# The first two token tiles' norm weights applied at the PSUM exit, and the last block's squares moved to row tiles

## The chip, the cores and the metric

The kernel runs on one NeuronCore of a Trainium2 chip, as one launch. The metric is the device time in microseconds, the median of several runs of the same program. Beside those runs one execution was recorded by the hardware profiler; its rows carry the argument. TensorE multiplies matrices into PSUM, VectorE (DVE in the rows) and ScalarE (ACT) take results out of PSUM and prepare operands, GpSimd (POOL) works on SBUF, and SyncE (SP) issues most of the transfers.

## The reference

One encoder layer over 2048 tokens of width 1024, in fp32, with root-mean-square norms around every part. Cut to what matters here:

```python
def rms_norm(x, g):
    y = xf * lax.rsqrt(jnp.mean(xf * xf, axis=-1, keepdims=True) + RMS_EPS)
    return (y * g.astype(jnp.float32)).astype(x.dtype)
...
u = rms_norm(h, g_mix_pre[l])
z = u @ w_in[l]
...
u = rms_norm(h, g_ffn_pre[l])
y = (jax.nn.silu(u @ w_gate[l]) * (u @ w_up[l])) @ w_down[l]
h = h + rms_norm(y, g_ffn_post[l])
```

Between the two quoted parts stand sliding-window attention, a gated linear recurrence, an output projection and a cross-attention into 256 memory tokens. The change touches the first norm (`g_mix_pre`) at the start of the kernel and the last norm (`g_ffn_post`) at its end.

## The kernel before

**Numbers.** Each fp32 operand of a product is split in two parts that TensorE multiplies fast: "hi" is the value rounded by a copy, "lo" is the value minus hi. A product is then three matmuls: hi by hi, hi by lo, lo by hi (lines 1131 to 1133). So each tile that enters a product costs one copy (ScalarE or GpSimd, line 987 or 989) and one subtraction on VectorE (line 990).

**The start (`in_first`).** The first products are the input projection of 512 tokens. Tokens come in tiles of 128 rows, `x0_0` tiles 0 to 3 and `x0_1` tiles 4 to 7. For each tile, `scaled` calls `normed`: ScalarE squares the rows and sums them (line 429; the squares go to a scratch tile), GpSimd makes the reciprocal root in two small instructions (lines 102 and 104), and VectorE multiplies the tile by it and by the norm weights, which lie broadcast over 128 partitions in the tile `g` (line 431). Then TensorE transposes the tile in eight pieces of 128x128 into two PSUM banks (`flipped`, line 480), after which the model width lies on the partitions. `first` takes the two banks out: ScalarE writes hi (line 497), VectorE lo (line 498). `copied` writes the plain transposed values to `raw` as well (line 486, ScalarE), because a later step of the block product (sums of quarters) needs them unsplit. Meanwhile TensorE turns over the identity matrix (`turns`, line 449), 36 times before tile 0 and 18 times before tile 1. The first products (of kind "q") take tiles 0 and 1 together, 256 columns a matmul, then tiles 2 and 3.

SyncE's queue at the start is: tile 0, the broadcast weights, tile 1, two pieces of the first projection weights (`sraw`), tiles 2 and 3, two more pieces of weights, tiles 4 and 5, and so on.

**The middle.** Block products of 2x2 blocks of 512 columns with seven products instead of eight (`seven`: the steps are numbered 1, 5, 6, 3, 7, 2, 4), an addend kept in a "part" tile (three buffers of 128x512), and operands that stream in from HBM.

**The end (`down_block`).** The last product of the feed-forward part makes 256 tokens at a time, two row tiles of 128x1024 in four halves (i, j). In the last block (`end`), `out` does for each half: an addition out of PSUM (lines 1721 to 1723), a sum of squares on ScalarE (`mean_square`, line 1504, with its scratch tile taken from the same three "part" buffers), and a multiplication by the norm weights on VectorE (line 1730). When both halves of a row tile are there, GpSimd adds the two sums (line 1733) and takes the root (line 1736), VectorE multiplies and adds the residual in two halves (line 1739), and each half is stored.

**Order.** The code is traced in program order, and the framework then lists each engine's instructions in the order in which a simulation of the kernel finds them ready; dependences become semaphore waits. `queued(...)` and `traced(...)` pin the start's order by hand: what stands in the block is issued after the named instruction. In the built program's list the four halves at the end leave PSUM in the order (0,0), (0,1), (1,1), (1,0), while ScalarE squares them in the order (0,1), (1,1), (0,0), (1,0).

Tiles of 128x1024 of the late stages come from a pool with twelve buffers (`row_tile`); small constants come from the pool `cst`, which lies below all other tiles of its side.

Of the kernel before, what the change touches and what calls it, by code (L numbers as in the profile page):

```python
# [11 lines left out]
F32 = mybir.dt.float32  # L12
F32R = mybir.dt.float32r
I32 = mybir.dt.int32
AF = mybir.ActivationFunctionType
ALU = mybir.AluOpType
AX = mybir.AxisListType

P = 128
# [5 lines left out]
KT = D // P  # L25
# [5 lines left out]
EPS = 1e-6  # L31
# [5 lines left out]
def f32(ap):  # L37
    return ap.bitcast(F32)
# [10 lines left out]
class Layer:  # L49
# [372 lines left out]
        self._n += 1  # L422
        return self.st_pool.tile([P, 2, D], F32, tag="pair", name=f"pair_{self._n}", bufs=5)

    def normed(self, x, junk, *at):
        nc = self.nc
        ss = self.small("n_s")
        with self.queued(*at):
            nc.scalar.activation(junk, x, AF.Square, accum_out=ss)
            r = self.rstd([ss], D, "n")  # L430
            nc.vector.scalar_tensor_tensor(x, x, r, self.g_mix, ALU.mult, ALU.mult)

    def traced(self, engine):

# [16 lines left out]
    def in_first(self):  # L451

        nc, I = self.nc, self.I
        stage = []

        def x_loads(s, tiles):
            if tiles[0] == 0:
                stage.append(self.tb.tile([P, 4, D], F32, tag="T", name=f"x0_{s}", bufs=3))
            for i in tiles:
                self.load(stage[s][:, i, :], I["x"][(4 * s + i) * P:(4 * s + i + 1) * P, :])  # L460
                if s + i == 0:
                    self.g_mix = self.gain(I["g_mix_pre"])

        x_loads(0, (0, 1))
        T, raw = {}, {}
        key = {(0, 0): 1, (1, 0): 2, (0, 1): 8, (1, 1): 3}

        def scaled(s, i, *at):
            junk = stage[0][:, i % 2, :] if s else raw[0, 1].rearrange("p k t -> p (k t)")[:, 0:D]
            self.normed(stage[s][:, i, :], junk, *at)  # L470

        def flipped(s, i, kinds):

            x = stage[s][:, i, :]
            banks = []
            for q in range(2):
                ps = self.bank(kinds[q])
                for j in range(4):
                    k = 4 * q + j
                    nc.tensor.transpose(ps[:, j * P:(j + 1) * P], x[:, k * P:(k + 1) * P], self.ident)  # L480
                banks.append(ps.rearrange("p (j t) -> p j t", j=4))
            return banks

        def copied(s, i, banks):
            for q in range(2):
                nc.scalar.activation(raw[q, s][:, :, i * P:(i + 1) * P], banks[q], AF.Copy)

        def parts(s, i, q):
            o = slice(i * P, (i + 1) * P)
            return T[key[q, s]][:, 0, :, o], T[key[q, s]][:, 1, :, o]  # L490

        def first(i, kinds):

            banks = flipped(0, i, kinds)
            for q in range(2):
                hi, lo = parts(0, i, q)
                nc.scalar.activation(hi, banks[q], AF.Copy)
                nc.vector.tensor_tensor(lo, banks[q], f32(hi), ALU.subtract)
            return banks

        def later(i, *at):
            scaled(1, i, *at)
            banks = flipped(1, i, ("sh", "gt")[i % 2])
            copied(1, i, banks)
            for q in range(2):
                self.split2(raw[q, 1][:, :, i * P:(i + 1) * P], *parts(1, i, q), "P")
# [10 lines left out]
        def fetch():  # L517
            for s in range(2):
                for q in range(2):
# [8 lines left out]
        tokens = [[] for _ in range(len(self.ORDER) + 1)]  # L528
        blocks = [("s",) + self.in_block(*p, tokens[i], tokens[i + 1], beside[i + 1], get if i > 9 else (), i < 2,
                                         None if i else lambda: x_loads(0, (2, 3)))  # L530
                  for i, p in enumerate(self.ORDER)]

# [4 lines left out]
        PE, ACT, DVE, POOL = (getattr(mybir.EngineType, e) for e in ("PE", "Activation", "DVE", "Pool"))  # L537
        next(phases)
        self.turns("h", 36)
        x_loads(1, (0, 1))  # L540
        scaled(0, 0)
        b0 = first(0, "sh")
        a0 = self.traced(ACT)
        with self.queued(self.traced(PE)):
            self.turns("g", 18)
        scaled(0, 1)
        with self.queued(self.traced(POOL), self.traced(DVE)):
            next(phases)
        b1 = first(1, "gt")
# [3 lines left out]
        x_loads(1, (2, 3))  # L553
        scaled(0, 2, a0, v1)
        scaled(0, 3, a1)
        with self.queued(self.traced(ACT)):
            copied(0, 0, b0)
        b2 = first(2, "gt")
        a2 = self.traced(ACT)
        with self.queued(self.traced(PE)):  # L560
# [1 line left out]
        b3 = first(3, "sh")  # L562
# [1 line left out]
        with self.queued(self.traced(PE)):  # L564
            next(phases)
        with self.queued(a3):
            for i, b in ((1, b1), (2, b2), (3, b3)):
                copied(0, i, b)
        with self.queued(a3, v3):
            next(phases)  # L570
# [15 lines left out]
        for s in range(2):  # L586
            u.append([])
            for q in range(2):
                self._n += 1
                t = self.big.tile([P, 2, 4, 512], F32R, tag="big", name=f"u1_{q}{s}")  # L590
                r = second[q, s]
# [905 lines left out]
        return lambda kind: self.streamed(lambda t, j: self.load(  # L1497
            t, src[n:n + 2, j].rearrange("i p c -> p i c")), 4, kind, "A", tiles=True, blocked=True)

    def mean_square(self, a, to):  # L1500

        self._n += 1
        junk = self.st_pool.tile([P, 512], F32, tag="part", name=f"junk_{self._n}", bufs=3)
        self.nc.scalar.activation(junk, a, AF.Square, scale=float(D) ** -0.5, accum_out=to)  # L1504

    def mean_squares(self, y, i, ss):
# [186 lines left out]
    def down_block(self, c, f0, nk, n):  # L1693
        nc = self.nc
        last = f0 + 2 * nk == NFF
        end = last and n == NT - 2
        late = last and n >= NT - 4
        y, x, ss = {}, {}, []

        def stream(kind):  # L1700
            if late:
                for i in range(2):
                    y[i] = self.rows_of(self.y2_d, n + i)
            if last and n == 0:
                self.g_post = self.gain(self.I["g_ffn_post"])
            return self.streamed(lambda t, j: self.load(
                t, self.h_d[f0 + j * nk:f0 + (j + 1) * nk, :, n * P:(n + 2) * P].rearrange("k p t -> p k t")),
                nk, kind, "A")

        def part(i, j):  # L1710
            return y[i][:, j * 512:(j + 1) * 512]

        def out(i, j, a, b):
            if i not in y:
                y[i] = self.row_tile()
            if end and not x:
                for r in range(2):
                    x[r] = self.rows_of(self.h2_d, n + r)
            d = part(i, j)
            if b is not None:  # L1720
                nc.vector.tensor_tensor(d, a, b, ALU.add)  # L1721
            elif late:
                nc.vector.tensor_tensor(d, a, d, ALU.add)
            else:
                nc.scalar.activation(d, a, AF.Copy)
            if end:
                if not ss:
                    ss.append(self.small("q_s", 4))
                self.mean_square(d, ss[0][:, 2 * i + j:2 * i + j + 1])
                nc.vector.tensor_tensor(d, d, self.g_post[:, j * 512:(j + 1) * 512], ALU.mult)  # L1730
                if (i, 1 - j) in seen:
                    v = self.small("p_v")
                    nc.gpsimd.tensor_scalar(v, ss[0][:, 2 * i:2 * i + 1], ss[0][:, 2 * i + 1:2 * i + 2], EPS,
                                            ALU.add, ALU.add)
                    r = self.small("p_r")
                    nc.gpsimd.tensor_tensor(r, v, self.mhalf[:, 0:1], ALU.pow)
                    for q in range(2):
                        sl = slice(q * 512, (q + 1) * 512)
                        nc.vector.scalar_tensor_tensor(y[i][:, sl], y[i][:, sl], r, x[i][:, sl], ALU.mult, ALU.add)
                        self.store(self.out[(n + i) * P:(n + i + 1) * P, sl], y[i][:, sl])  # L1740
                seen.append((i, j))

        seen = []

        def after():
            if end:
                return
            s2 = self.small("q_s", 4) if last else None
            for i in range(0 if late else 2):
                if not c:  # L1750
                    self.store(self.y2_d[(n + i) * P:(n + i + 1) * P, :], y[i])
                elif last:
                    self.add(y[i], self.y2_d, n + i)
                else:
                    self.add_to(self.y2_d, n + i, y[i])
                yield
            if last:
                if not late:
                    yield
                for i in range(2):  # L1760
                    self.mean_squares(y[i], i, s2)
                yield
                r = self.rstds(s2)
                for i in range(2):
                    nc.vector.scalar_tensor_tensor(y[i], y[i], r[:, i:i + 1], self.g_post, ALU.mult, ALU.mult)
                    self.add_to(self.out, n + i, y[i])
                    yield

        return stream, out, after, part if late else None


# [19 lines left out]
```

## Time and profile before

| | |
|---|---|
| median of 3 runs | 2552.73 us (2552.61 to 2555.01) |
| the profiled execution, its own time | 2550.01 us |
| its span | 2548.3 us, 34324 instructions, granted clock 0.997 |
| TensorE busy | 2504.8 us, 98% of the span |
| VectorE busy | 1792.1 us, 70% |
| ScalarE busy | 1261.6 us, 50% |
| GpSimd busy | 364.6 us, 14% |
| moved by DMA | 486.33 MB, mean 191 GB/s |

A row of the profile gives the engine, the line of the code, the operation, the tiles it writes and reads by their names in the program, the shapes, and the time. "Idle before" is the time in which the engine had nothing to do, followed by the instruction or the transfer that ended it. Matmuls overlap in the array, so one lasts longer than the distance to the next. A busy engine that nobody waits for costs nothing, and an idle one that is not the last to be ready doesn't either.

### The profile page before, as it was taken

How to read it: one execution, taken by the hardware profiler on the slowest of the kernel's cores; microseconds unless marked ns; L12 is line 12 of the kernel's file. 1: busy time of each engine (PE TensorE's matmuls, PEld its weight loads, DVE VectorE, ACT ScalarE, POOL GpSimd, SP SyncE). 2: the span in 40 equal slices, each digit the busy share in tenths (PEclk: the TensorE clock that was granted, in tenths of full speed). 3: DMA queues.
4: the chain of work that ended last, by engine and by line, in shares of the span. 5: the costliest groups of instructions: out<-in, count | busy, mean ns of one | idle time of the engine just before them, and what ended most of it. 6: DMA issues, size and time to landing. Idle time of an engine off the chain costs nothing.

```text
span 2548.3 us, 34324 instructions
## 1 busy us (share of the span) xinstructions
PE 2504.8 (98%) x12006; PEld 2092.8 (82%) x12006; DVE 1792.1 (70%) x2871; ACT 1261.6 (50%) x2635; POOL 364.6 (14%) x540
## 2 busy tenths in 40 slices
PE   9999999999999999999999999999999999999998
PEld 8878888877997778878878888888888888878886
DVE  8885488987556989988876555576566557574766
ACT  5553466655555566566753333353333335443543
POOL 4231234321311112102200000000000000000022
PEclk9999999999999999999999999999999999999999
DMA  6455655865887996867954522254465434564786
GB/s 201 146 165 178 192 154 170 230 204 146 259 292 275 316 335 189 274 206 226 333 200 146 177 91 87 74 203 148 160 210 195 144 117 159 180 188 106 228 177 151
DMA packets 387885, 486.33 MB, mean 191 GB/s; under 512 B 22272, under 2 KB 283392, under 8 KB 387712
## 3 DMA queue, kind: packets, MB, share of 16 engines
q1 hardware_dynamic: 381664, 462.12, 55.9%
q0 software_dynamic: 6048, 22.02, 5.0%
q8 instruction: 94, 1.54, 0.2%
q14 instruction: 79, 0.65, 0.1%
HBM read 317.34 MB, written 166.72 MB: 190 GB/s over the span
## 4 chain that ended last, share of the span: by engine, by line
PE 51%; DVE 2%; DMA 1%; issue 1%; ACT 1%; POOL 0%; SPq 0%; DVEq 0%; POOLq 0%; ACTq 0%
PE psm L1133 17%; PE psm L1131 17%; PE psm L1132 17%; DVE T L990 0%; DVE S L990 0%; ACT junk L1504 0%; PE pss L1390 0%; DMA out_dram<-row 0%; DMA row<-d_s 0%; DMA row<-in_w_down_dram 0%; DMA u_d<-row 0%; DMA sraw<-in_w_gate_dram 0%; DVE sum L1106 0%; ACT S L987 0%; ACT T L987 0%
## 5 line engine op out<-in xcount | busy, mean ns | idle before, releaser
L1131 PE MATMUL psm<-T,S 128*128 128x512 f32 x2680 | 1034.1, 390 | 13.3 <-ACT part L1146 7.2
L1132 PE MATMUL psm<-T,S 128*128 128x512 f32 x2680 | 1042.3, 390 | 4.0 <-DVE T L990 3.9
L1133 PE MATMUL psm<-T,S 128*128 128x512 f32 x2680 | 1029.4, 389 | 4.1 <-DVE S L990 4.1
L1131 PEld LDWEIGHTS psm<-T,S 128*128 128x128 f32 x2680 | 503.0, 188 | 125.9 <-ACT part L1146 11.9
L1132 PEld LDWEIGHTS psm<-T,S 128*128 128x128 f32 x2680 | 503.2, 188 | 110.5 <-DVE T L990 7.3
L1133 PEld LDWEIGHTS psm<-T,S 128*128 128x128 f32 x2680 | 503.1, 188 | 110.6 <-DVE S L990 6.3
L987 ACT ACTIVATE S<-sum 128x512 fp32r<-128x512 f32 (+1 forms) x370 | 224.0, 620 | 371.5 <-PE psm L1133 267.3
L990 DVE TENSOR_TENSOR S<-sraw,S 128x512 fp32r<-128x512 f32 (+1 forms) x315 | 211.5, 679 | 218.8 <-ACT S L987 215.8
L1146 ACT ACTIVATE part<-psm 128x512 f32<-128x512 f32 x285 | 168.6, 596 | 251.9 <-PE psm L1133 230.9
L990 DVE TENSOR_TENSOR S<-sum,S 128x512 fp32r<-128x512 f32 (+1 forms) x388 | 257.4, 673 | 42.1 <-ACT S L987 38.3
L987 ACT ACTIVATE S<-sraw 128x512 fp32r<-128x512 f32 (+1 forms) x300 | 184.7, 618 | 110.8 <-PE psm L1133 106.0
L1537 POOL DMA_DIRECT2D y_d<-row x16 | 14.1, 879 | 1077.9 <-DVE row L1721 1027.6
L990 DVE TENSOR_TENSOR T<-row,T 128x1024 fp32r<-128x1024 f32 (+1 forms) x112 | 131.0, 1183 | 30.2 <-ACT T L987 29.2
L157 PE MATMUL psg<-u,whi 128*128 128x512 f32 x320 | 128.3, 401 | 0.0
L158 PE MATMUL psg<-u,wlo 128*128 128x512 f32 x320 | 127.6, 399 | 0.0
L156 PE MATMUL psg<-u,whi 128*128 128x512 f32 x320 | 127.5, 399 | 0.0
L1504 ACT ACTIVATE junk<-row 128x512 f32<-128x512 f32 x160 | 99.6, 624 | 40.6 <-DVE row L1526 20.6
L987 ACT ACTIVATE T<-row 128x1024 fp32r<-128x1024 f32 (+1 forms) x112 | 113.3, 1031 | 7.5 <-DMA row<-d_s 4.3
L1672 DVE TENSOR_TENSOR row<-psm,part 128x512 f32<-128x512 f32 x66 | 43.7, 687 | 66.9 <-PE psm L1133 66.9
L1681 DVE TENSOR_TENSOR part<-psm,part 128x512 f32<-128x512 f32 x66 | 43.8, 687 | 60.1 <-PE psm L1133 59.8
L1721 DVE TENSOR_TENSOR row<-psm,part 128x512 f32<-128x512 f32 x72 | 49.1, 688 | 49.5 <-PE psm L1133 49.4
L814 ACT ACTIVATE S<-S,w_mn 128x256 f32<-128x256 f32 (+1 forms) x128 | 63.0, 496 | 29.6 <-DVE w_mn L810 29.2
(363 smaller groups left out, 3562.2 us busy)
## 6 DMA issues: line engine op xcount, KB each, us to landing
sraw<-in_w_gate_dram SPq DMA_DIRECT2D x44, 512.0 KB, 3.6
sraw<-in_w_up_dram SPq DMA_DIRECT2D x44, 512.0 KB, 3.7
hid_d<-row SPq DMA_DIRECT2D x44, 512.0 KB, 2.7
sraw<-hid_d SPq DMA_DIRECT2D x32, 512.0 KB, 4.2
sraw<-in_w_in_dram SPq DMA_DIRECT2D x44, 256.0 KB, 4.0
z_d<-pair SPq DMA_DIRECT2D x20, 512.0 KB, 3.4
raw<-in_w_in_dram SPq DMA_DIRECT2D x20, 512.0 KB, 4.8
z_d<-z SPq DMA_DIRECT2D x20, 512.0 KB, 4.0
```

The costliest lines, as they stand in the source:

```text
L156: nc.tensor.matmul(ps, ah, bh, start=(i == 0), stop=False)
L157: nc.tensor.matmul(ps, ah, bl, start=False, stop=False)
L158: nc.tensor.matmul(ps, al, bh, start=False, stop=(i == n - 1))
L814: nc.scalar.activation(s[:, r, o:], s[:, r, o:], AF.Exp, bias=mn[:, i:i + 1], scale=-1.0, accum_out=den[:, i:i + 1])
L987: self.nc.scalar.activation(hi, raw, AF.Copy)
L990: self.nc.vector.tensor_tensor(lo, raw, f32(hi), ALU.subtract)
L1131: nc.tensor.matmul(ps, s[:, 0, k, :], t[:, 0, k, :], start=st, stop=False, **kw)
L1132: nc.tensor.matmul(ps, s[:, 0, k, :], t[:, 1, k, :], start=False, stop=False, **kw)
L1133: nc.tensor.matmul(ps, s[:, 1, k, :], t[:, 0, k, :], start=False, stop=sp, **kw)
L1146: nc.scalar.activation(t, ps, AF.Copy)
L1504: self.nc.scalar.activation(junk, a, AF.Square, scale=float(D) ** -0.5, accum_out=to)
L1721: nc.vector.tensor_tensor(d, a, b, ALU.add)
```

## The change

At the start: `normed` can leave the weights out; tiles 0 and 1 are then multiplied by their reciprocal root alone. Their weights come in as `g_col`, eight numbers on each of the 128 partitions, gathered by a transfer of single elements, and VectorE multiplies each PSUM bank of these two tiles by them on its way out, into `raw`; hi and lo are made from `raw`, and the separate copies to `raw` go. The broadcast weights `g`, which tiles 2 and up still use, are loaded behind tile 1 instead of behind tile 0.

At the end: in the last block the scratch tile of the squares is a row tile of its own, and the addition of the two sums of squares and the epsilon runs on VectorE.

```diff
-    def normed(self, x, junk, *at):
+    def normed(self, x, junk, *at, gains=True):
...
-            nc.vector.scalar_tensor_tensor(x, x, r, self.g_mix, ALU.mult, ALU.mult)
+            if gains:
+                nc.vector.scalar_tensor_tensor(x, x, r, self.g_mix, ALU.mult, ALU.mult)
+            else:
+                nc.vector.tensor_scalar_mul(x, x, r)
...
-                if s + i == 0:
+                if s == 0 and i == 0:
+                    self.g_col = self.cst.tile([P, KT], F32, name="g_col")
+                    self.load(self.g_col, I["g_mix_pre"].rearrange("r (k p) -> p (r k)", p=P))
+                if s == 0 and i == 1:
                     self.g_mix = self.gain(I["g_mix_pre"])
...
-            self.normed(stage[s][:, i, :], junk, *at)
+            self.normed(stage[s][:, i, :], junk, *at, gains=s or i > 1)
...
-                nc.scalar.activation(hi, banks[q], AF.Copy)
-                nc.vector.tensor_tensor(lo, banks[q], f32(hi), ALU.subtract)
+                a = banks[q]
+                if i < 2:
+                    a = raw[q, 0][:, :, i * P:(i + 1) * P]
+                    nc.vector.tensor_tensor(a, banks[q], self.g_col[:, 4 * q:4 * q + 4].unsqueeze(2)
+                                            .broadcast_to([P, 4, P]), ALU.mult)
+                nc.scalar.activation(hi, a, AF.Copy)
+                nc.vector.tensor_tensor(lo, a, f32(hi), ALU.subtract)
...
-        with self.queued(self.traced(ACT)):
-            copied(0, 0, b0)
...
-            for i, b in ((1, b1), (2, b2), (3, b3)):
+            for i, b in ((2, b2), (3, b3)):
                 copied(0, i, b)
...
-    def mean_square(self, a, to):
+    def mean_square(self, a, to, junk=None):
-        junk = self.st_pool.tile([P, 512], F32, tag="part", name=f"junk_{self._n}", bufs=3)
+        if junk is None:
+            junk = self.st_pool.tile([P, 512], F32, tag="part", name=f"junk_{self._n}", bufs=3)
...
-                self.mean_square(d, ss[0][:, 2 * i + j:2 * i + j + 1])
+                self.mean_square(d, ss[0][:, 2 * i + j:2 * i + j + 1], self.row_tile()[:, 0:512])
...
-                    nc.gpsimd.tensor_scalar(v, ss[0][:, 2 * i:2 * i + 1], ss[0][:, 2 * i + 1:2 * i + 2], EPS,
+                    nc.vector.tensor_scalar(v, ss[0][:, 2 * i:2 * i + 1], ss[0][:, 2 * i + 1:2 * i + 2], EPS,
                                             ALU.add, ALU.add)
```

## The prediction

> **What bounds the kernel now.** I read first how busy TensorE is by stretch, then the start and the end of the run in order of time, engine by engine. In the first view a row is a stretch of the span, with busy time and instruction count of each engine, granted clock, share of the DMA engines' time, and GB/s.
>
> ```profile
> 0.00:13.28 13.28, 10.59 (x71) 9.91 (x71) 4.92 (x7) 7.08 (x12) 3.52 (x15) 1.00 0.89 283
> 13.28:100.00 86.72, 86.10 (x447) 73.62 (x448) 73.52 (x96) 44.07 (x78) 33.95 (x43) 1.00 0.59 176
> 100.00:2500.00 2400.00, 2369.48 (x11322) 1977.88 (x11321) 1681.93 (x2726) 1195.80 (x2512) 314.89 (x465) 1.00 0.61 192
> 2500.00:2539.56 39.56, 38.68 (x170) 31.43 (x168) 27.72 (x40) 13.90 (x33) 10.87 (x16) 1.00 0.61 113
> 2539.56:2548.30 8.74, 0.00 (x0) 0.00 (x0) 4.01 (x6) 0.72 (x2) 1.36 (x2) 0.66 0.32 120
> ```
>
> TensorE is busy 2369.48 of the middle 2400.00 us. Only three things can shorten this kernel without taking matmuls away: the 13.28 us before the first product, the 8.74 us after the last one, and the 30.52 us of waits between. The change works on the first two. Here is the start, TensorE first, then ScalarE, then VectorE (start, duration, engine, line, operation; in brackets the idle time before it and what ended it).
>
> ```profile
> 1.49 6.44 PE L449 MATMUL pss<-ident 128*128 128x128 f32 x36 [1.49 <-POOL ident masks.py:199]
> 8.24 1.09 PE L480 MATMUL pss<-ident,x 128*128 128x128 f32 x8 [0.32 <-DVE x L431]
> 14.24 0.38 PE L1132 MATMUL psm<-u,S 128*128 128x256 f32 x1 [0.49 <-DVE u L498]
> 19.28 1.04 PE L480 MATMUL pss<-ident,x 128*128 128x128 f32 x8
> ```
>
> ```profile
> 4.79 1.06 ACT L429 ACTIVATE pair<-x 128x1024 f32<-128x1024 f32 x1 [2.72 <-DMA x<-in_x_dram]
> 8.04 1.06 ACT L429 ACTIVATE pair<-x 128x1024 f32<-128x1024 f32 x1 [2.10 <-DMA x<-in_x_dram]
> 14.55 1.09 ACT L486 ACTIVATE pair<-pss 128x512 f32<-128x512 f32 x2
> ```
>
> ```profile
> 6.90 1.28 DVE L431 SCALAR_TENSOR_TENSOR x<-x,n_r,g 128x1024 f32<-128x1024 f32 x1 [5.97 <-POOL n_r L104]
> 9.71 0.69 DVE L498 TENSOR_TENSOR u<-pss,u 128x512 fp32r<-128x512 f32 x1 [1.53 <-ACT u L497]
> 10.32 1.47 DVE L431 SCALAR_TENSOR_TENSOR x<-x,n_r,g 128x1024 f32<-128x1024 f32 x1
> 11.71 1.28 DVE L990 TENSOR_TENSOR S<-sraw,S 128x512 fp32r<-128x512 f32 x2
> 12.92 0.68 DVE L498 TENSOR_TENSOR u<-pss,u 128x512 fp32r<-128x512 f32 x1
> 13.52 1.27 DVE L498 TENSOR_TENSOR u<-psm,u 128x512 fp32r<-128x512 f32 x2
> 14.71 1.41 DVE L431 SCALAR_TENSOR_TENSOR x<-x,n_r,g 128x1024 f32<-128x1024 f32 x1
> 17.25 1.27 DVE L431 SCALAR_TENSOR_TENSOR x<-x,n_r,g 128x1024 f32<-128x1024 f32 x1
> ```
>
> From 14.24 TensorE runs on. What it waited for there is VectorE's "lo" part of tile 1 (the first of the pair at 13.52, done near 14.15). VectorE has no gap from 9.71 to that point, so VectorE, and not the load of tile 1, sets when the products begin.
>
> The end, TensorE, ScalarE, VectorE, GpSimd. L1721 and L1723 take finished sums out of PSUM, L1504 squares them, L1730 multiplies by the norm weights, L1733 and L1736 make the reciprocal root, and L1739 finishes the row.
>
> ```profile
> 2536.58 0.47 PE L1131 MATMUL psm<-T,S 128*128 128x512 f32 x1 [0.88 <-DVE row L1721]
> 2539.17 0.39 PE L1133 MATMUL psm<-T,S 128*128 128x512 f32 x1
> ```
>
> ```profile
> 2533.80 0.63 ACT L1504 ACTIVATE junk<-row 128x512 f32<-128x512 f32 x1 [7.01 <-issue]
> 2537.15 0.62 ACT L1504 ACTIVATE junk<-row 128x512 f32<-128x512 f32 x1
> 2541.50 0.63 ACT L1504 ACTIVATE junk<-row 128x512 f32<-128x512 f32 x1 [3.64 <-DVE row L1723]
> ```
>
> ```profile
> 2530.64 0.68 DVE L1721 TENSOR_TENSOR row<-psm,part 128x512 f32<-128x512 f32 x1
> 2535.75 0.69 DVE L1721 TENSOR_TENSOR row<-psm,part 128x512 f32<-128x512 f32 x1 [0.50 <-PE psm L1133]
> 2539.45 1.42 DVE L1739 SCALAR_TENSOR_TENSOR row<-row,p_r,row 128x512 f32<-128x512 f32 x2 [0.87 <-POOL p_r L1736]
> 2540.78 0.68 DVE L1723 TENSOR_TENSOR row<-psm,row 128x512 f32<-128x512 f32 x1
> 2542.26 0.69 DVE L1730 TENSOR_TENSOR row<-row,g 128x512 f32<-128x512 f32 x1 [0.79 <-ACT junk L1504]
> 2543.80 1.41 DVE L1739 SCALAR_TENSOR_TENSOR row<-row,p_r,row 128x512 f32<-128x512 f32 x2 [0.86 <-POOL p_r L1736]
> ```
>
> ```profile
> 2542.32 0.79 POOL L1733 TENSOR_SCALAR p_v<-q_s 128x1 f32<-128x1 f32 x1 [2.91 <-ACT junk L1504]
> 2543.20 0.57 POOL L1736 TENSOR_TENSOR p_r<-p_v,mhalf 128x1 f32<-128x1 f32 x1
> ```
>
> The last product ends at 2539.17 + 0.39 = 2539.56, but its eviction (L1723) starts at 2540.78: VectorE is closing row tile 0 (L1739, two instructions from 2539.45). That is late because one half of row tile 0, out of PSUM at 2530.64, is squared only at 2537.15: the square's scratch tile comes from the three "part" buffers, which the unfinished sums still hold, so the squares stand in a line behind each other.
>
> **The change, part by part: the start.** These rows price what the trace does not have: two 4 KB gathers by single elements (size and median us from issue to landing), and small multiplications by a per-partition number.
>
> ```profile
> gx<-in_g_x_pre_dram SPq DMA_DIRECT2D x1, 4.0 KB, 4.5
> lb<-in_hgrn_lb_dram SPq DMA_DIRECT2D x1, 4.0 KB, 9.1
> ```
>
> ```profile
> L1600 DVE TENSOR_SCALAR row<-row,mc x64: 323/346/355, 974.3 to 1104.7; 128x256 f32<-128x256 f32 x64
> L373 DVE TENSOR_SCALAR fa<-mc x1: 155/155/155, 43.4 to 43.4; 128x4 f32<-128x4 f32 x1
> L102 POOL TENSOR_SCALAR n_v<-n_s x18: 192/192/1284, 6.0 to 573.1; 128x1 f32<-128x1 f32 x18
> ```
>
> *Loads.* Tile 0 lands by 4.79 and tile 1 by 8.04, with the broadcast weights between them: 512 KB each, so (8.04 - 4.79) / 2 = 1.6 us apiece. With the broadcast behind it, tile 1 lands at 6.4, plus the gather's share. The gather is issued about where the weights were, near 1.2; by the first row it lands near 5.7, so its share is 0 to 0.9, and I take 0.3: tile 1 at 6.7. By the second row, which had a long queue ahead, it would land at 10.3, past its first use at 8.5; I take the first, since here one transfer is ahead. SP issues one DMA more; every later transfer is some 0.3 us later, and the broadcast lands near 8.3, long before tile 2 is scaled at 14.71.
>
> *Scaling.* The two 128x1024 passes of L431 become multiplications by one number a row. From (0.346 - 0.155) / 252 elements, 1024 take 0.155 + 0.78 = 0.93 (estimate; ends 0.35, the 256-wide row, and 1.28, the old pass). For tile 0 that ends at 7.83, but TensorE's warm-up runs to 1.49 + 6.44 = 7.93, so tile 0's transposes move from 8.24 only to 7.95, and their first bank is full near 8.5. [...]
>
> *Weights at the PSUM exit.* Four new VectorE passes of 128x512 out of PSUM, 0.63 each by the pair at 13.52. Counted from 8.5 to the "lo" part that TensorE waits for: four new passes 2.52 (the fourth fills the wait for ScalarE's "hi" of tile 1), scaling of tile 1 0.93, both weights' lo 1.28, tile 0's two lo 1.26, tile 1's first lo 0.63: 6.6, ending at 15.1 against 14.15, +1.0. If the two weights' lo and one of tile 0's stand behind it, 13.2, -0.9. In the trace the weights' lo ran ahead (11.71) and tile 0's second lo late (12.92); with that one behind, 14.5. I take +0.4. Behind it VectorE stays late: 1.2 earlier start, 2.5 more, 0.5 less, so tile 3's scaling ends 0.8 later than 18.52, at 19.3; tile 3's transposes, shifted, would start at 19.7. That cover of 0.4 is all there is.
>
> *Copies dropped.* Four ScalarE copies (L486) of 0.55 go. TensorE waits for none of them in this stretch: nothing.
>
> **The end.** With scratch tiles of their own, the square of the half that left PSUM at 2530.64 can run at 2531.4, so row tile 0's last square is that of 2533.80, and its closing pair starts near 2536.0 instead of 2539.45. Row tiles cannot run short: twelve buffers, six in use, four more. Then L1723 starts at 2539.60 instead of 2540.78: -1.18. What is late next is the chain behind it, which stays: square, root, closing pair, store.
>
> *The sum on VectorE.* From square to closing pair now takes 2543.80 - 2541.50 = 2.30. Afterwards: 0.76 to L1730, 0.62 for it, 0.16 for the sum (L373), 0.65 for the root with its hand-over, 0.03: 2.22, so -0.08. If the sum is put ahead of L1730, 1.60, -0.70. The sum's 0.79 on GpSimd beside L1730, against 0.192 in the median elsewhere (L102), shows that GpSimd is held up while VectorE runs such a pass. [...] I take -0.08. The sum waits for ScalarE, and behind it in VectorE's queue stand, for row tile 0, the eviction at 2535.75, for which TensorE waits; that is a rival below.
>
> Sum: +0.4 - 1.18 - 0.08 = -0.9. The profiled execution took 2550.01 us, so 2549.1; the runs' median is 2552.73, 2.7 above it, so I predict 2551.9. Differences under 0.2% (5.1 us) are about what a measurement of this kernel can tell from no change.
>
> **Rivals.**
> *Both ends go well.* Tile 1's lo comes before the weights' lo (-0.9), and the sum goes ahead of L1730 without the root being held (-1.88): -2.8, 2549.9 on the median. For it: 1.5 us of earlier data; against it: the order at 11.71, and the 0.79.
> *VectorE is late at both ends: slower.* The start costs the full +1.0. At the end row tile 0's closing pair, ready near 2536.0, is listed ahead of the eviction that ran at 2535.75; that one then runs at 2537.4, and the last four accumulations start 1.65 later: -1.26 + 1.65 = +0.4. Together +1.4, 2554.1. It decides on a quarter of a microsecond in VectorE's list. For it: 73.52 of 86.72 us busy after the start; against it: the eviction is listed first in the code.
> *The gather lands late.* At 10.3 by the lb row, the first new pass waits 1.8 us: +2.2 at the start, +0.9 in all, 2553.6.
> *The middle is re-ordered.* The list of each engine is made from simulated times, so a shift at the start can change it later, and the new constant moves the addresses above it. The place is the 30.52 us of waits; a sixth of them gone or added is 5.1 us, 2547.6 or 2557.8. For it: many waits under a microsecond; against it: the same work and dependences.
>
> **How the numbers follow.** Forecast 0.40, both ends well 0.18, late VectorE 0.14, late gather 0.04, middle faster 0.14, middle slower 0.10. So faster by over 0.2% 0.14, within 0.2% 0.76, slower 0.10. The range runs from 2546.5 (half of the faster middle) to 2555.5 (late VectorE, and the gather's bound, with 1.4 for the middle); 0.17 is left out. The likeliest case alone has 2550.8 to 2553.
>
> **What would show it.** Right: Square of tile 1 near 6.7; first L1132 within 13.3 to 15.2; no gap over 0.5 at tile 3's transposes; L1504 for the first half near 2531.4 on the old scale; the last eviction within 0.1 us of the last matmul; 7.5 us after it. Wrong: a first new pass that waits for the gather; a closing pair ahead of the eviction of row tile 1; a middle whose waits differ from 30.5 by more than 3 us.

## The result, and the profile after

The changed kernel took 2556.86 us (median of 22 runs) against 2552.73 for the kernel before in the same session: ratio 1.0018, 95% interval 1.0012 to 1.0024. That is 3.1 to 6.1 us slower. The ratio lies inside the 0.2% that I called no change (its interval reaches a little beyond), but the time is 1.4 us above my range. Its profiled execution took 2558.76 us, with a span of 2557.0.

First the view by stretch, columns as before; the last row runs from the last product to the end of the span.

```profile
0.00:13.28 13.28, 9.85 (x70) 9.14 (x70) 3.95 (x7) 5.18 (x8) 2.90 (x13) 1.00 0.87 263
13.28:100.00 86.72, 82.98 (x426) 71.70 (x427) 74.02 (x96) 41.98 (x73) 29.02 (x41) 0.96 0.57 172
100.00:2500.00 2400.00, 2365.34 (x11304) 1974.09 (x11303) 1682.15 (x2725) 1192.44 (x2505) 317.75 (x466) 1.00 0.61 191
2548.53:2557.00 8.47, 0.00 (x0) 0.00 (x0) 4.02 (x7) 0.72 (x2) 0.55 (x1) 0.65 0.33 124
```

The second row holds the loss: TensorE is busy 3.1 us less than before in the same stretch (82.98 against 86.10), and the granted clock is 0.96 where it was 1.00. The end shrank from 8.74 to 8.47 only. Now the start in order of time: TensorE, ScalarE, VectorE.

```profile
7.49 1.09 PE L486 MATMUL pss<-ident,x 128*128 128x128 f32 x8 [0.30 <-DVE x L434]
...
16.00 0.77 PE L1140 MATMUL psm<-u,S 128*128 128x256 f32 x2 [4.24 <-POOL S L998]
17.79 0.58 PE L1141 MATMUL psm<-u,S 128*128 128x256 f32 x1 [1.01 <-DVE u L509]
18.16 0.41 PE L1142 MATMUL psm<-u,S 128*128 128x256 f32 x1
18.38 0.41 PE L1140 MATMUL psm<-u,S 128*128 128x256 f32 x1
```

```profile
7.76 1.06 ACT L429 ACTIVATE pair<-x 128x1024 f32<-128x1024 f32 x1 [2.03 <-DMA x<-in_x_dram]
11.66 0.63 ACT L996 ACTIVATE S<-sraw 128x512 fp32r<-128x512 f32 x1 [2.75 <-DMA sraw<-in_w_in_dram]
```

```profile
6.68 0.75 DVE L434 TENSOR_SCALAR x<-x,n_r 128x1024 f32<-128x1024 f32 x1 [5.74 <-POOL n_r L104]
9.86 0.75 DVE L434 TENSOR_SCALAR x<-x,n_r 128x1024 f32<-128x1024 f32 x1 [2.43 <-POOL n_r L104]
10.53 0.68 DVE L506 TENSOR_TENSOR pair<-pss,g_col 128x512 f32<-128x512 f32 x1
11.50 0.69 DVE L999 TENSOR_TENSOR S<-sraw,S 128x512 fp32r<-128x512 f32 x1 [0.29 <-POOL S L998]
...
14.51 1.28 DVE L506 TENSOR_TENSOR pair<-psm,g_col 128x512 f32<-128x512 f32 x2
16.03 0.69 DVE L999 TENSOR_TENSOR S<-sraw,S 128x512 fp32r<-128x512 f32 x1 [0.23 <-POOL S L998]
16.64 1.10 DVE L509 TENSOR_TENSOR u<-pair,u 128x512 fp32r<-128x512 f32 x1
```

Tile 0 is transposed 0.75 us earlier, and then nothing more is gained. Tile 1's square starts at 7.76, only 0.28 earlier than before (8.04), and the first weights' parts (11.66) 1.64 later than the 10.02 of before. VectorE idles 2.43 us for tile 1's root, because its list has tile 1's multiplication ahead of tile 0's passes (L506), whose data has been in PSUM since 8.58 (7.49 + 1.09). TensorE's first product of all comes at 16.00 instead of 13.28, released by GpSimd's part of the weights, and the first one that needs a "lo" part at 17.79 instead of 14.24. And from there products of 256 columns are 0.21 us apart instead of 0.12: the granted clock is 0.50 from 14.94 to 21.77, by this row.

```profile
14.94:21.77 6.83, 4.75 (x20) 4.49 (x21) 6.51 (x8) 2.27 (x4) 4.28 (x6) 0.50 0.99 316
```

The 101st of the block's products is a fixed mark behind all this. It stands at 30.00 before and at 35.30 after:

```profile
30.00 0.39 PE L1132 MATMUL psm<-u,S_u 128*128 128x512 f32 x1
```

```profile
35.30 0.39 PE L1141 MATMUL psm<-u,S_u 128*128 128x512 f32 x1
```

So the start costs 5.30: 3.55 until the first product that needs a "lo", and 1.75 behind it (17.51 from there to the mark, against 15.76). At the end, ScalarE and VectorE:

```profile
2542.76 0.63 ACT L1514 ACTIVATE row<-row 128x512 f32<-128x512 f32 x1 [7.01 <-issue]
2545.43 0.63 ACT L1514 ACTIVATE row<-row 128x512 f32<-128x512 f32 x1 [1.94 <-DVE row L1731]
2546.06 0.62 ACT L1514 ACTIVATE row<-row 128x512 f32<-128x512 f32 x1
2550.36 0.63 ACT L1514 ACTIVATE row<-row 128x512 f32<-128x512 f32 x1 [3.59 <-DVE row L1733]
```

```profile
2539.60 0.68 DVE L1731 TENSOR_TENSOR row<-psm,part 128x512 f32<-128x512 f32 x1
...
2548.31 1.42 DVE L1749 SCALAR_TENSOR_TENSOR row<-row,p_r,row 128x512 f32<-128x512 f32 x2 [0.69 <-POOL p_r L1746]
2549.64 0.68 DVE L1733 TENSOR_TENSOR row<-psm,row 128x512 f32<-128x512 f32 x1
...
2552.59 1.42 DVE L1749 SCALAR_TENSOR_TENSOR row<-row,p_r,row 128x512 f32<-128x512 f32 x2 [0.67 <-POOL p_r L1746]
```

The half that left PSUM at 2539.60 is still squared third, at 2546.06, though its scratch is now a row tile. ScalarE idles 7.01 us ahead of its first square here, for which the profile names no releaser ("issue"). That first square is of another half, which left PSUM only at 2542.68 (an eviction of 0.69 us from 2541.99), so it is the order of ScalarE's list, rather than a buffer, that seems to hold the early half; the last two runs below test this. The last eviction (2549.64) still stands 1.11 us behind the last product's end at 2548.53.

Start and end make 5.30 - 0.27 = +5.0; the medians say 4.1 (3.1 to 6.1). The span of this profile is 8.7 above the one before: the rest is mostly waits between 600 and 900 us, where two profiled executions differ anyway (below).

### The profile page after: what moved, and what is told of

It reads as the page before. It is cut to its first block, busy times and chain, and to the rows that moved or that the text cites. A ratio compares the mean times of both kernels' runs of the same rounds, so it can differ in the third digit from the quotient of the medians.

```text
span 2557.0 us, 34323 instructions
## 1 busy us (share of the span) xinstructions
PE 2505.8 (98%) x12006; PEld 2093.8 (82%) x12006; DVE 1796.1 (70%) x2877; ACT 1258.8 (49%) x2631; POOL 361.4 (14%) x538
## 3 DMA queue, kind: packets, MB, share of 16 engines
q8 instruction: 94, 1.54, 0.2%
## 4 chain that ended last, share of the span: by engine, by line
PE 51%; DVE 2%; issue 1%; ACT 1%; DMA 1%; SPq 0%; POOL 0%; DVEq 0%; POOLq 0%; ACTq 0%
PE psm L1142 17%; PE psm L1140 17%; PE psm L1141 17%; DVE T L999 1%; DVE S L999 0%; ACT junk L1514 0%; PE pss L1399 0%; DMA out_dram<-row 0%; ACT T L996 0%; DMA row<-in_w_down_dram 0%; DVE sum L1115 0%; DMA row<-d_s 0%; DMA u_s<-row 0%; DVE row L1644 0%; ACT S L996 0%
```

## Experiments

Ratios are to the kernel before, run on the same chip, with 95% intervals. "Mark" is the 101st product (30.00 before, 35.30 after); "tail" runs from the last product's end to the span's end (8.74 and 8.47).

| kernel | ratio | mark | tail |
|---|---|---|---|
| end alone | 0.9996 [0.9985, 1.0007] | 29.96 | 8.59 |
| start alone | 1.0018 [1.0008, 1.0028] | 36.27 | 8.70 |
| rows instead of gather | 1.0015 [1.0006, 1.0024] | 35.67 | |
| passes pinned | 1.0025 [1.0016, 1.0035] | 36.68 | |
| TensorE kept busy | 1.0010 [1.0001, 1.0019] | 33.28 | |
| squares in banks | 1.0002 [0.9993, 1.0011] | | 7.48 |
| load order alone | 1.0001 [0.9992, 1.0009] | 30.66 | |
| column of ones | 1.0025 [1.0014, 1.0035] | 35.28 | |
| gather on ScalarE's queue | 1.0013 [1.0004, 1.0022] | 35.20 | |
| all three costs out | 1.0001 [0.9993, 1.0010] | 32.38 | |
| early square and end | 0.9995 [0.9985, 1.0005] | 29.91 | 7.54 |
| early square alone | 1.0000 [0.9991, 1.0009] | | 7.58 |

**The two halves of the change.** The start alone, and the end alone:

```
# end alone: only these two edits on the kernel before
+ self.mean_square(d, ss[0][:, ...], self.row_tile()[:, 0:512])
+ nc.vector.tensor_scalar(v, ...)      # was nc.gpsimd
```

> The kernel before with the end's two edits alone (squares into row tiles, the sum on VectorE); the start as before. Theory 1 (the loss is made at the start, the end gains little): first dense product at 14.2 us as before, last product to the span's end 8.47 +- 0.1 us against 8.74, ScalarE squares the (0,0) half last but one as before, and the time is within 0.5 us of before. Theory 2 (the edits at the end re-order the middle): TensorE's waits between come to about 42 us instead of 34, and the time is 2 to 4 us above before. My prediction on record has this part at -1.26.

> The kernel before with the start's edits alone (tiles 0 and 1 loaded first, weights at the PSUM exit, gather of the weights by element); the end as before. Theory 1: the start carries the loss: first dense product at 17.8 instead of 14.24, granted clock at one half for some 7 us from 15, products at 110 us of the span 4.8 us behind before, last product to the end 8.74; time +4.4 us against before (3.5 to 5.5). Theory 2 (the middle or the end carries it): start +1 or less in the time, total below +2.

The end alone is within its interval of before, the start alone carries the whole ratio. In the profile of the end alone TensorE's waits (those over 0.12 us) between 600 and 900 us add up to 13.7 us, against 10.1 before and 14.2 after, and its time can't be told from before's. So a difference of that size in one profiled execution isn't evidence of a loss; that the start also shifts the middle a little is neither shown nor excluded. (All waits between 100 and 2500 us come to 30.2 to 33.3 us in the six profiles with the old start and to 31.7 to 35.7 in the eight with the new one, so a small shift is likely, but no run isolates it.)

The start alone also shows how far two profiles of the same start differ. Its first product that needs a "lo" comes at 17.77, as in after, but its half clock begins at 17.05 instead of 14.94, so that nearly all of it falls on products: from there to the mark it takes 18.50, 2.74 more than before where after has 1.75 more.

**Is it the gather by elements?** Eight rows of 512 bytes, turned by TensorE:

```
- self.load(self.g_col, I["g_mix_pre"].rearrange("r (k p) -> p (r k)", p=P))
+ self.load(g_rows, I["g_mix_pre"].rearrange("r (k p) -> (r k) p", p=P))
...
+ nc.tensor.transpose(ps[:, 0:KT], g_rows, self.ident[0:KT, 0:KT])
+ nc.scalar.activation(self.g_col, ps[:, 0:KT], AF.Copy)
```

> The kernel after, but the column of weights is no longer gathered by 1024 elements: eight rows of 512 bytes are loaded and TensorE turns them (one small transpose, one small ScalarE copy). Theory 1 (the gather takes about 1.65 us of SyncE's DMA queue from every later load): tile 1 lands at 6.0 to 6.4 instead of 7.67, tile 2 at 11.3 instead of 12.94, VectorE scales tile 1 at 8.3 to 8.6 instead of 9.86, and with the list as it is the first dense product comes at 16.2 to 16.6 instead of 17.79: 1.2 to 1.6 us back. Theory 2 (two 512 KB loads in a row cost that by themselves): tile 1 lands at 7.4 to 7.7 as in after and nothing comes back.

ScalarE, square of tile 1 and first weights' part:

```profile
8.45 1.06 ACT L429 ACTIVATE pair<-x 128x1024 f32<-128x1024 f32 x1 [2.66 <-DMA x<-in_x_dram]
...
12.10 0.64 ACT L1001 ACTIVATE S<-sraw 128x512 fp32r<-128x512 f32 x1 [2.44 <-DMA sraw<-in_w_in_dram]
```

Both are later than in after (7.76, 11.66), so the number of elements isn't what costs. So the next two runs took the small transfer away in two ways:

```
# load order alone, on the kernel before        # column of ones, on the kernel after
-    if s + i == 0:                             - self.load(self.g_col, ...)
+    if s == 0 and i == 1:                      + nc.gpsimd.memset(self.g_col, 1.0)
         self.g_mix = self.gain(...)
```

> The kernel before with one edit: the two first tiles are loaded ahead of the broadcast weights; no gather, the weights applied in the old pass. It tells whether the later landing of tile 1 and of all that follows comes from the gather or from the order of the big loads. Theory 1 (the small transfer between costs it, of whatever shape): tile 1 lands at 6.2 to 6.6, the broadcast at 7.9 to 8.2, tile 2 at 11.2 to 11.4 as before. Theory 2 (the order costs it): tile 1 at 7.6 to 8.0 and tile 2 at 12.7 to 13. By either, tile 0's scaling waits for the broadcast and the first dense product comes at 15 or later; time +0.5 to +3 against before.

> The kernel after without the load of the weight column: GpSimd writes ones into it, so tiles 0 and 1 get no norm weights; all passes stay. Theory 1 (the small transfer costs 1.65 us of the queue): tile 1 lands at 6.0 to 6.6, tile 2 at 11.3, the second pair of the first weights at 13.5 and 14.4, and the first dense product comes near 16.2. Theory 2 (the order of the large loads): landings as in after (7.67, 12.94, 15.1, 16.0) and the first dense product at 17.5 to 17.9. Its list also puts the parts of the first weights ahead of tile 0's passes on VectorE, which by itself moves no more than 0.3.

ScalarE of the column of ones:

```profile
5.98 1.06 ACT L429 ACTIVATE pair<-x 128x1024 f32<-128x1024 f32 x1
...
10.12 0.63 ACT L996 ACTIVATE S<-sraw 128x512 fp32r<-128x512 f32 x1 [2.99 <-DMA sraw<-in_w_in_dram]
```

Tile 1's square starts at 5.98 and the first weights' part at 10.12; the load order alone, with the same loads ahead, has 6.21 and 10.58. Against these two, a transfer of 4 KB puts tile 1's square back by 1.55 to 1.78 us and the weights by 1.08 to 1.54 as a gather, by 2.24 to 2.47 and 1.52 to 1.98 as rows. The start alone, passes pinned and TensorE kept busy issue the same loads as after and have tile 1's square at 8.05, 8.01 and 7.64, so such a price is known to about 0.4 us. As a gather the 4 KB cost tile 1 about what a load of 512 KB does (1.6, by the prediction's rows), as rows more; no run shows why. Yet with ones, which leave the norm weights of tiles 0 and 1 out, the first product with a "lo" part comes at 17.40, not at 16.2 as I expected; its list put the weights' parts ahead of tile 0's passes:

```profile
10.79 0.69 DVE L999 TENSOR_TENSOR S<-sraw,S 128x512 fp32r<-128x512 f32 x1 [0.56 <-ACT S L996]
11.40 1.28 DVE L506 TENSOR_TENSOR pair<-pss,g_col 128x512 f32<-128x512 f32 x2
```

Early data alone brought 0.39 us here, since the list made the passes wait for something else.

**The gather on another queue.**

```
- self.load(self.g_col, ...)               # SyncE's queue
+ nc.scalar.dma_start(self.g_col, ...)     # ScalarE's queue
```

> The kernel after, with the column of weights gathered through ScalarE's DMA queue instead of SyncE's; everything else as in after. In after (1024 elements) and with eight rows the small transfer put tile 1 1.5 us and all later loads 1.6 us back, without it they were on time. Theory 1 (the price is paid in SyncE's queue, by what stands behind the small transfer): tile 1 lands at 5.9 to 6.3, tile 2 at 11.3 to 11.9, VectorE scales tile 1 at 8.3; first dense product 16.2 to 16.6. Theory 2 (the small transfer holds up the DMA engines from any queue): tile 1 at 7.4 to 7.9, tile 2 at 12.7 to 13, first dense product at 17.5 to 17.9.

```profile
6.83 1.06 ACT L429 ACTIVATE pair<-x 128x1024 f32<-128x1024 f32 x1 [0.90 <-DMA x<-in_x_dram]
...
10.66 0.63 ACT L996 ACTIVATE S<-sraw 128x512 fp32r<-128x512 f32 x1 [2.68 <-DMA sraw<-in_w_in_dram]
```

Nearer to the first theory: tile 1 comes 0.93 earlier than in after and the weights 1.00; against the two kernels without the transfer 0.62 to 0.85 and 0.08 to 0.54 stay. The issue of the gather takes SyncE's queue 0.42 us by this row of after, and without it tile 1's own issue ends 0.62 us earlier; tile 1 gained 0.93, and over the four profiles with the gather on SyncE's queue (7.64 to 8.05) and the two on ScalarE's (6.83, and 6.71 in the run with all three costs out) it gained 0.81 to 1.34. So here the other queue saved more than the time to issue.

```profile
1.24 0.42 SPq L75 DMA_DIRECT2D g_col<-in_g_mix_pre_dram  x1
```

The first product with a "lo" part is 0.96 earlier than in after (16.83), but the mark is only 0.10 earlier: the half clock held for more of the products, which follow 0.21 us apart from 17.21 to 21.48 here, 21 of them against 17 in after.

**The order of VectorE's list.**

```
- scaled(0, 1)
+ scaled(0, 1, mul=passes)    # tile 1's multiplication queued behind tile 0's two passes
```

> The kernel after, with VectorE's scaling of tile 1 listed behind the two weight passes of tile 0. Theory 1 (the list's order put tile 0's passes behind a multiplication that waits for tile 1's load): the first pass starts at 8.1 instead of 10.53, the two passes (0.68 each) fill the 2.43 us of idle time, and the first dense product comes 1.2 to 1.4 us earlier, at 16.4 to 16.6; at full order price (all of the 2.0 us by which the first pass was late) at 15.8. Theory 2 (the load of tile 1 sets it, not the order): the first dense product stays at 17.6 to 17.9. Time 1.2 to 2 us below after by theory 1, 0 by theory 2.

VectorE, then GpSimd, then TensorE:

```profile
8.71 1.29 DVE L507 TENSOR_TENSOR pair<-pss,g_col 128x512 f32<-128x512 f32 x2 [1.18 <-PE pss L487]
...
17.12 0.69 DVE L1001 TENSOR_TENSOR S<-sraw,S 128x512 fp32r<-128x512 f32 x1 [0.51 <-POOL S L1000]
17.73 1.29 DVE L511 TENSOR_TENSOR u<-pair,u 128x512 fp32r<-128x512 f32 x2
```

```profile
16.10 0.99 POOL L1000 TENSOR_SCALAR S<-sraw 128x512 fp32r<-128x512 f32 x1 [0.21 <-DMA sraw<-in_w_in_dram]
```

The passes did move, from 10.53 to 8.71, into time that VectorE had idled. But the list then put both parts of the second weights ahead of tile 1's "lo", and their load, itself late, ends at 16: the "lo" starts at 17.73 instead of 16.64 and the first product that needs it comes at 18.47. Both theories missed: correcting one place of the order moved the wait to the next.

**The clock.**

```
  b1 = first(1, "gt")
+ with self.queued(self.traced(PE)):
+     self.turns("g", 30)      # idle transposes, nobody reads them
```

> The kernel after, with 30 more idle turns of the identity on TensorE behind the transposes of tile 1 (3.5 us of work that nobody reads), to fill the idle time before the first product. Theory 1 (the granted clock halves because TensorE idles for 4.2 us): no half clock from 15 us on, the first products 0.12 us apart instead of 0.21, some 1.3 us gained by 110 us of the span, the first dense product still at 17.8. Theory 2 (the half clock comes from elsewhere or costs nothing): clock or time as in after. Time 1.3 below after by theory 1.

```profile
12.00 3.44 PE L452 MATMUL psm<-ident 128*128 128x128 f32 x30
15.71 0.47 PE L1142 MATMUL psm<-u,S 128*128 128x256 f32 x2 [0.27 <-POOL S L1000]
17.49 0.39 PE L1143 MATMUL psm<-u,S 128*128 128x256 f32 x1 [1.31 <-DVE u L509]
17.72 0.28 PE L1144 MATMUL psm<-u,S 128*128 128x256 f32 x1
17.84 0.28 PE L1142 MATMUL psm<-u,S 128*128 128x256 f32 x1
```

Products follow at 0.12 us at once, and the mark is at 33.28: 2.02 earlier than in after, 0.30 of it from the earlier first product and 1.72 from the clock, close to the 1.75 counted above. At the start the half clock goes with the long wait: in after 6.83 us at 0.50 that begin within a wait of 4.24 us, and none where the wait was filled. Elsewhere it stands behind shorter waits: in before and in after the clock also falls to 0.50 twice in the middle, for 3.41 us each time. In before it does so at 279.3, where the longest wait in the 9 us ahead is 0.85 us, and at 630.9, behind one of 2.59; in after at 660.1, behind a wait of 2.79 us, and at 830.7, behind one of 1.72 us that stands in before too without such a fall. So a wait shorter than that of the start is no safeguard.

**All three at once.** Gather on ScalarE's queue, tile 1's transposes and passes traced ahead of the first weights' parts, 18 idle turns:

```
+ nc.scalar.dma_start(self.g_col, ...)
...
+ b1 = first(1, "gt")
+ with self.queued(self.traced(PE)):
+     self.turns("g", 18)
+ with self.queued(passes[1], passes[2]):
      next(phases)             # the first weights' parts
```

> The kernel after with all three suspected costs taken out: the gather on ScalarE's queue; tile 1's transposes and passes traced ahead of the first weights' parts, so that VectorE's list has tile 0's passes and lo parts ahead of the weights' lo; 18 idle turns on TensorE behind tile 1's transposes. Theory 1 (late loads, the list's order and the half clock make the whole loss; what is left is the extra VectorE work): first dense product at 14.3 to 15.3 at full clock, products at 110 us of the span within 0.5 to 1.2 us of before, time +0 to +1 against before. Theory 2 (the loss is the extra 2.5 us of passes, whatever their order): first dense product at 16.5 or later.

```profile
9.49 1.28 DVE L506 TENSOR_TENSOR pair<-pss,g_col 128x512 f32<-128x512 f32 x2
...
15.07 1.08 DVE L510 TENSOR_TENSOR u<-pair,u 128x512 fp32r<-128x512 f32 x1
```

```profile
16.21 0.39 PE L1144 MATMUL psm<-u,S 128*128 128x256 f32 x1 [1.57 <-DVE u L510]
```

The first such product comes at 16.21, between my two bounds, and the mark at 32.38: 2.92 of the 5.30 us are gone. Of the 2.38 that stay, 1.97 are there at that first product and go with VectorE's extra passes: from the first pass (9.49) to the end of the "lo" part (16.15) it has 6.7 us, with 0.69 of waiting, where before it took 4.4 from 9.71 on, tile 1's scaling included, and the wait of TensorE that ends last there is the one for this "lo". That is read from the rows; no run takes the passes away. In the whole time, ratio 1.0001 with an interval of 0.0017, this can't be told from before.

**The end: buffer or order?** First the squares' scratch in the PSUM bank just taken out, which needs no buffer. This version spoils one half of row tile 1, whose sum goes on in that bank; only its times are read.

```
- self.mean_square(d, ss[0][:, ...], self.row_tile()[:, 0:512])
+ self.mean_square(d, ss[0][:, ...], a)      # a: the bank
```

> The start of the kernel before; at the end the sum on VectorE, and the squares' scratch goes into the PSUM bank that has just been taken out, so that it needs no buffer from any pool. Theory 1 (in after and in the run with the end alone the list still waits for a row tile, whose buffer a store holds, so the early half of row tile 0 is squared last but one): here that half is squared first, right after its eviction near 2531.7, row tile 0's closing pair starts about 1.2 us or more earlier, the last eviction starts within 0.1 us of the last product, and last product to span's end is 7.2 to 7.5 us against 8.6 with row tiles and 8.74 before. Theory 2 (the order of ScalarE's list is set by the order in the code, not by buffers): still 8.4 to 8.7. Time 1.2 below before by theory 1.

The tail fell to 7.48, but the squares now also stand between products that add to one bank, which gives them another place in the list; the run could not tell buffer from order. Tracing the finished half first could:

```
+ def early(i, j, a, b):
+     if (i, j) in ((0, 1), (1, 1)):
+         held.append((i, j, a, b)); return
+     out(i, j, a, b)
+     while held:
+         out(*held.pop(0))
```

> The start of the kernel before; the end as in after, and besides the finished half (0,0) is traced ahead of (0,1) and (1,1), so that its square, first in the code, may be first in ScalarE's list. Theory 1 (the code's order held the square, not its scratch buffer): the half that leaves PSUM near 2531 is squared right behind that, row tile 0 is closed before the last product ends, the last eviction starts within 0.1 us of the last product's end, and from there 7.4 us to the span's end against 8.6 with the end's edits alone. Theory 2: 8.4 to 8.7. Time 1.2 below before by theory 1, which is less than its interval.

> The kernel before with that order of tracing alone: the squares' scratch stays in the three part buffers and the sum on GpSimd. Theory 1 (order alone): last product to span's end 7.5 to 7.6 against 8.74. Theory 2 (my prediction's: the scratch tile waits for a part buffer): the first square still waits for a buffer until 2533 or later, and 8.4 to 8.8 remain.

With the end's edits (VectorE):

```profile
2537.45 0.69 DVE L1722 TENSOR_TENSOR row<-psm,part 128x512 f32<-128x512 f32 x1 [0.42 <-PE psm L1133]
2538.06 1.41 DVE L1740 SCALAR_TENSOR_TENSOR row<-row,p_r,row 128x512 f32<-128x512 f32 x2
...
2541.30 0.69 DVE L1724 TENSOR_TENSOR row<-psm,row 128x512 f32<-128x512 f32 x1 [1.23 <-PE psm L1133]
```

The last eviction now waits for the last product (ended 2541.26) and starts 0.04 behind it, and the tail is 7.54. With the order alone (VectorE, then TensorE):

```profile
2538.27 1.41 DVE L1739 SCALAR_TENSOR_TENSOR row<-row,p_r,row 128x512 f32<-128x512 f32 x2 [0.86 <-POOL p_r L1736]
2539.60 0.68 DVE L1721 TENSOR_TENSOR row<-psm,part 128x512 f32<-128x512 f32 x1
```

```profile
2540.43 0.47 PE L1131 MATMUL psm<-T,S 128*128 128x512 f32 x1 [2.58 <-DVE row L1721]
```

The tail is 7.58 with the squares still in the three "part" buffers: the order in the code had held the square. But here the closing pair is listed ahead of the eviction, and TensorE waits 2.58 us for it where it had waited 0.88, so 1.70 are given back. And a half clock follows this wait as well (0.50 from 2541.4 on):

```profile
2544.03 0.63 PE L1132 MATMUL psm<-T,S 128*128 128x512 f32 x1
2544.46 0.56 PE L1133 MATMUL psm<-T,S 128*128 128x512 f32 x1
```

The last products are 0.43 us apart, where they are 0.23 apart in before, and from the end of the wait to the last product's end it takes 4.59 us instead of 2.98: 1.61 more. So the order alone gained 1.16 in the tail and lost 3.31 ahead of it. In the other version the sum on VectorE is listed between the squares and the closing pair, and the eviction goes first, as with the squares in banks; that it is the sum and not the squares' scratch that brings this about was not tested alone. That version, the kernel before with the end's edits and the early square, has the lowest ratio of those that ran: below after's (0.9995 against 1.0018, the intervals apart), not distinguishable from before.

## Why the prediction was wrong, step by step

The term that failed is the start's: +0.4, or +1.0 at the worst, where the first product that needs a "lo" came 3.55 later and the mark 5.30. Step by step:

- *Tile 1 at 6.7, with a share of 0.3 for the gather*: its square began at 7.76. The step took the gather's own landing as its price. It did land early, 3.7 us after its issue by the row below, but tile 1 behind it paid about 1.6 us. My bound of 0.9 was about half of that, and to the later loads I had charged 0.3 where they paid 1.1 to 1.5.

```profile
g_col<-in_g_mix_pre_dram SPq DMA_DIRECT2D x1, 4.0 KB, 3.7
```

- *First pass at 8.5*: 10.53. I counted the passes from the moment their bank was full and never asked what stood ahead of them in VectorE's list. This is the largest part of the 3.55: 2.03 us. Moving the passes forward by itself gained nothing (passes pinned), because what stood behind them in the list then waited.
- *6.6 us of VectorE work, 14.5 at the likeliest, 15.1 at the worst*: from the first pass to the end of the "lo" part it was 7.21, where my count without the scaling has 5.7. The difference is one more part of the weights ahead of the "lo" (0.61), two waits for GpSimd (0.29 and 0.23), and the "lo" itself at 1.10 instead of 0.63 while GpSimd ran beside it. With the list in order it was 6.7, still 1.0 above that 5.7: a wait of 0.69 for ScalarE's "hi", and again the longer "lo".
- *The clock* was no term at all. TensorE idled for 4.24 us ahead of its first product, and the half clock that followed cost 1.75 more (2.74 in the start alone).
- *Multiplication 0.93*: 0.75, by the row at 6.68. It gained nothing, since the list spent it waiting.
- *Copies dropped at nothing; tile 3's cover of 0.4*: no row contradicts either; TensorE has no wait over 0.12 us between 17.8 and 112 us.
- *-1.18 at the end*: what follows from an early square was foreseen rightly (by the order alone the tail went from 8.74 to 7.58), what held the square was not. The squares stood in the order of the code, in "part" buffers or row tiles alike, so the edit itself brought none of it.
- *-0.08 for the sum on VectorE*: from the last square to the closing pair it is 2552.59 - 2550.36 = 2.23 against 2.30: right. Row tile 0's closing gains about as much. In after the sum stands behind the multiplication by the norm weights both times (2551.72 behind 2551.11); whether the root would be held with the sum ahead of it, and the -0.70 be lost, is not shown.
- *Rivals.* The late VectorE was the right sign at the start, with 1.0 where 3.55 and a half clock came. Its other half, the closing pair listed ahead of the eviction and 1.65 us lost for TensorE, did not come in after; it came in the early square alone, at 1.70 and a half clock of 1.61 behind it. The gather did not land late, and no pass waited for it.
- *The middle*: its waits went from 30.5 to 34.7, more than the 3 us that I named, but the end alone has 33.3 at an unchanged time. The two times that I gave for it, 2547.6 and 2557.8, also leave out the -0.9 of the sum; with it they are 2546.8 and 2557.0.

## What to carry to other kernels

When a step is added to an engine's list, find out what will be listed ahead of it and what that waits for; the time its data is ready is only a lower bound (here 8.58 against 10.53). Charge a small load with what it does to the loads behind it (here 0.8 to 2.5 us), not with its own landing, and keep it off the queue whose next load is awaited (on ScalarE's queue tile 1 came 0.81 to 1.34 earlier). Where a change makes TensorE wait, look for a half clock behind the wait and add its price: here it added a half to the price of a late start (1.75 to 3.55), and at the end it outweighed the gain (1.61 against 1.16).

## What the runs showed of the hardware

- One 4 KB transfer ahead of the large ones put these back by 0.8 to 2.1 us as 1024 elements (four profiles) and by 1.5 to 2.5 as eight rows (one profile); on ScalarE's queue by 0.9 at most (two profiles). Why eight rows cost no less than 1024 elements stays open.
- Behind an idle time of TensorE of 3.23 to 4.24 us before the first products (after, rows, passes pinned, column of ones, gather on ScalarE's queue) products of 256 columns came 0.21 us apart instead of 0.12, and in after the half clock lasted 6.83 us. Its price at the mark was 1.75 (after) to 2.74 us (start alone), depending on which work it fell on: with the gather on ScalarE's queue the first product that needs a "lo" led after by 0.96 us, and the mark by 0.10.
- Shorter waits were followed by a half clock in some cases and not in others: 2.59 us in before was (3.41 us at 0.50), 2.58 us at the end of the early square alone was (products 0.43 us apart instead of 0.23), 2.33 us at the start of the load order alone was not; 1.72 us was in after and was not in before. What decides it stays open.
- A "lo" pass of 128x512 took 1.08 to 1.10 us instead of 0.68 where GpSimd made a weights' part beside it (after, rows, TensorE kept busy, gather on ScalarE's queue, all three costs out). The weights' pass that started at 16.03 in after, also beside GpSimd, took 0.69; what decides it stays open.
